# High and low fp32r parts for the product of attention weights with V, query tiles in pairs, masks on GpSimd, and GEMM tiles at low SBUF offsets

## The chip, the cores and the metric

The kernel runs on one core of one Trainium2 chip. The metric is the device time of one execution in microseconds (us); less is better. The core has a matrix engine (TensorE, PE in the profile, with its weight loads as PEld), three elementwise engines (VectorE or DVE, ScalarE or ACT, GpSimd or POOL), a queue engine for transfers (SyncE, SP), an on-chip memory of 128 partitions (SBUF) and the matrix engine's output memory (PSUM, in banks of 128 x 512 float32).

## The reference, cut to what matters

Two layers work on a residual stream x of 512 tokens x 1024 features. Layer 0 mixes tokens with stick-breaking attention, layer 1 with a gated linear recurrence (HGRN2); each is followed by an MLP with squared ReLU. All is float32.

```python
def stick_breaking_attention(q, k, v):
    ...
    for t0 in range(0, seq, Q_BLOCK):                       # query tiles of 128
        t1 = t0 + Q_BLOCK
        z = jnp.einsum('bhqd,bhkd->bhqk', q[:, :, t0:t1], k[:, :, :t1]).astype(jnp.float32) * scale
        causal = jnp.arange(t1)[None, :] < (t0 + jnp.arange(Q_BLOCK))[:, None]
        log_stay = jnp.where(causal, jax.nn.log_sigmoid(-z), 0.0)
        log_between = lax.cumsum(log_stay, axis=3, reverse=True) - log_stay
        weights = jnp.where(causal, jnp.exp(jax.nn.log_sigmoid(z) + log_between), 0.0)
        outs.append(jnp.einsum('bhqk,bhkd->bhqd', weights.astype(v.dtype), v[:, :, :t1]))
...
def squared_relu_mlp(h, w1, w2):
    a = jax.nn.relu(h @ w1)
    return (a * a) @ w2
...
    for layer in range(DEPTH):                              # 2 layers
        h = rmsnorm(x, norm_gains[layer, 0])
        x = x + (stick_breaking_mixer if layer == 0 else hgrn2_mixer)(h, ...)
        h = rmsnorm(x, norm_gains[layer, 1])
        x = x + squared_relu_mlp(h, mlp_w1[layer], mlp_w2[layer])
```

There are 16 attention heads of 64 features; the last line of the loop, attention weights times V, is what the change rewrites.

## The kernel before, in words

**GEMMs on split numbers.** Each large product is made of three fp32r products: an operand is split into a high part (rounded to fp32r) and a low part (the rest), and high x high, high x low and low x high are summed in PSUM. Normed activations are the tiles `xh`, `xl` (tag `P`, 16 buffers of 2 KB a partition), hidden activations `hh`, `hl` and attention outputs `oh`, `ol` (tag `Q`, 16 buffers). Weights come in slabs of 1 MB: two transfers of 512 KB on SP's queue into `wr`, then ACT rounds each half to `wh` (L263) and DVE subtracts to get `wl` (L264), one slab ahead of the matrix engine. Projections with tokens in the output's rows (`gemm_x`) stream 256 weight columns a matmul; those with features in the rows (`gemm_w`) stream 512 tokens.

**Attention.** Four groups g of four heads. In a group the main thread makes q, k (two slabs), norms them, then makes V (a third slab, L533). Two tasks `prepare_pair` transpose q and k and split them (`kst`, `qh`, `ql`); four tasks `head` follow. A head has four query tiles T = 0..3, each of W = 128 (T + 1) keys, and three kinds of step:

- `z_of(T)`: scores `z` by two matmuls, ACT's two sigmoids `sn` and `sg` (L588, L589), a reversed running product over `sn` on DVE (L591), and `sg *= sn` on DVE (L595).
- `turn(T)`: T + 1 transposes of `sg` into PSUM `pa`, and the way back to SBUF `at`: DVE's product with the mask `before` (L610) on the diagonal block, for T > 1 ACT's copy (L609) of the others.
- `apply(T)`: T + 1 float32 matmuls (two passes each in the trace) with 64 columns of V as weights, into the head's half of the partitions of `po`. One PSUM bank `av` holds `po` for the pair; after the second head `split_out` makes `oh`, `ol` (L340, L341).

**What sets the order.** Matmuls are issued in an order fixed by hand: a small planner (`Line`) keeps a clock of nominal matmul times and lets up to three tasks push their steps in between the main thread's GEMM, with the lags in the table `LAG`. DVE, ACT and POOL take the order that the scheduler derives; each engine runs its queue strictly in order. After attention comes `project` (output projection in two parts: part 0 needs heads 0 to 7 and runs beside the last heads, part 1 needs all), then the MLP in four rounds of an up phase (moving tiles `xh`, `xl`) and a down phase (moving tiles `hh`, `hl`), 192 matmuls each.

Of the kernel before, what the change touches and what calls it, by code (L numbers as in the profile page):

```python
# [16 lines left out]
P = 128  # L17
# [13 lines left out]
def level_columns(H, skip):  # L31
# [27 lines left out]
def trunk(  # L59
# [20 lines left out]
    wp = ctx.enter_context(tc.tile_pool(name="wp", bufs=2))  # L80
    ap = ctx.enter_context(tc.tile_pool(name="ap", bufs=2))
# [3 lines left out]
        "P": 16, "Q": 16, "X5": 2, "R4": 4, "B": 2, "qT": 13, "sn": 2, "AT": 3, "sq": 2, "bc": 1,  # L85
# [4 lines left out]
    def sb(tag, shape=(P, S), dt=F32, name=None):  # L90
        return ap.tile(list(shape), dt, tag=tag, bufs=BUFS[tag], name=name or tag)
# [77 lines left out]
    rows = sb("AT", (40, P), name="rows")  # L169
# [6 lines left out]
    def gain(layer, j, kt):  # L176
# [10 lines left out]
    before = cp.tile([P, 2 * P], F32, name="before")  # L187
# [7 lines left out]
    nc.vector.memset(before, 1.0)  # L195
    nc.gpsimd.affine_select(
        out=before[:, P:], in_=before[:, P:], pattern=[[1, P]], compare_op=ALU.is_gt,
        fill=0.0, base=0, channel_multiplier=-1,
    )
    def late_constants():  # L200
        nc.vector.tensor_mul(gqk, gq, gk)
# [45 lines left out]
    def slab_halves(spec):  # L247
# [168 lines left out]
    def attention(norm):  # L416
# [74 lines left out]
        for g in range(4):  # L491
# [27 lines left out]
            vs = []  # L519
            for pair in range(2):  # L520
                shared = {"po": None}
# [4 lines left out]
            V = sb("B", (P, TT, SLAB), name="V")  # L526
            for hf in range(2):
                p = ps("mm")
                for u in range(2):
                    yield from gemm_x(p[:, u * SLAB : (u + 1) * SLAB], wsl, 2 * hf + u, acts)  # L530
                for u in range(2):
                    t = 2 * hf + u
                    nc.scalar.activation(  # L533
                        out=V[:, t, :], in_=p[:, u * SLAB : (u + 1) * SLAB], func=AF.Copy,
                        scale=r[:, t : t + 1],
                    )
            vs.append(V)
        return outs, heads

    live = {"sg": 0}  # L540
# [28 lines left out]
    def head(ready, vs, pair, j, shared, outs, slot):  # L569
# [3 lines left out]
        hc = (2 * pair + j) * SB_DH  # L573
# [6 lines left out]
        def z_of(T):  # L580
# [13 lines left out]
            )  # L594
            nc.vector.tensor_tensor(  # L595
# [3 lines left out]
        at = [None] * TT  # L599

        def turn(T):
            W = (T + 1) * P
# [3 lines left out]
            at[T] = sb("AT", name="at")  # L606
            lead = W - P if T > 1 else 0
            if lead:
                nc.scalar.copy(at[T][:, :lead], p[:, :lead])  # L609
            nc.vector.tensor_mul(at[T][:, lead:W], p[:, lead:W], before[:, 2 * P - (W - lead) :])  # L610

        def apply(T):
            if shared["po"] is None:
                shared["po"] = ps("av", name="po")
            o = blk(shared["po"], T)[j * SB_DH : (j + 1) * SB_DH, :]
            for b in range(T + 1):
                mm(o, vs[0][:, b, hc : hc + SB_DH], blk(at[T], b), b == 0, b == T)

        for step in LAG["head"]:
            if isinstance(step, float):  # L620
                yield step
            else:
                kind, T = step
                while kind == "a" and not vs:
                    yield 0.5
                {"z": z_of, "t": turn, "a": apply}[kind](T)
                if step == ("t", TT - 1):
                    live["sg"] -= 1
        if j == 1:
            outs[slot] = split_out(shared["po"])  # L630
# [304 lines left out]
    def mix(sc, task, V, G, j, outs, slot):  # L935
# [30 lines left out]
        og = sb("AT", name="og")  # L966
# [11 lines left out]
    def store(m, t0, n):  # L978
# [4 lines left out]
        o = sb("AT", name="o")  # L983
# [102 lines left out]
```

## Time and profile before

| | before |
|---|---|
| time, median of 3 runs | 1324.25 us (1322.35 to 1326.43) |
| profiled execution: time / span | 1325.41 us / 1323.7 us |
| PE busy / DVE / ACT / POOL, share of the span | 98% / 60% / 34% / 6% |
| granted matrix clock, mean | 0.996 |
| DMA | 110.64 MB, mean 84 GB/s |

The span is the time from the first to the last instruction of the profiled execution. A busy matrix engine is not one at its peak, since matmuls overlap in the record: what a matmul costs is read from the distance between the starts of successive ones, not from its duration. Rows of a window give, for each engine, its busy time in the window and the number of instructions.

### The profile page before, as it was taken

Reading aid. Unit: us, or ns where it says so; the run is one execution under the profiler, and the core shown is the slowest. Engines: PE = TensorE matmul, PEld = TensorE weight load, DVE = VectorE, ACT = ScalarE, POOL = GpSimd, SP = SyncE. Lnnn points to the kernel's source line nnn. Section 1 sums busy time; section 2 is a strip of 40 time slices with the busy share of each in tenths; the row PEclk is TensorE's granted clock in tenths of the full one; section 3 lists DMA queues with packets and bytes.
Section 4 is the critical chain, followed back from the end, with each engine's and each line's share of the span. In section 5 each row is a group of like instructions: output and inputs, shape, how many; then the busy total and the mean of one; then the engine's idle time right before and its main releaser. Section 6 shows DMA issues by size and latency. Waiting matters only on the chain.

```text
span 1323.7 us, 17619 instructions
## 1 busy us (share of the span) xinstructions
PE 1300.2 (98%) x6993; PEld 1104.2 (83%) x6993; DVE 798.7 (60%) x1534; ACT 446.0 (34%) x756; POOL 80.0 (6%) x139
## 2 busy tenths in 40 slices
PE   7999999999999999999999999999999999999998
PEld 7989898778888888888888888888888888888887
DVE  5787687867535435345578888797764353453441
ACT  5554454544212222123333333342432221221221
POOL 0100000000000000000013222232000000000000
PEclk8999999999999999999999999999999999999999
DMA  5312121113333333333321222221333333333331
GB/s 178 108 33 65 33 68 61 49 48 96 96 96 96 96 96 96 96 96 96 96 89 47 88 64 65 64 65 64 96 96 96 96 96 96 95 96 94 97 96 48
DMA packets 110657, 110.64 MB, mean 84 GB/s; under 512 B 3848, under 2 KB 106416, under 8 KB 110576
## 3 DMA queue, kind: packets, MB, share of 16 engines
q1 hardware_dynamic: 110496, 109.22, 26.7%
q8 instruction: 55, 0.90, 0.3%
q0 software_dynamic: 80, 0.31, 0.1%
q14 instruction: 26, 0.21, 0.0%
HBM read 107.41 MB, written 2.10 MB: 83 GB/s over the span
## 4 chain that ended last, share of the span: by engine, by line
PE 84%; DVE 10%; POOL 2%; issue 2%; ACT 1%; SPq 1%; DMA 1%; DVEq 0%; POOLq 0%; ACTq 0%
PE ps_mm L151 70%; PE po L151 3%; PE ps_z L151 3%; POOL tot L812 2%; DVE sc L845 2%; PE ps_s L151 2%; DVE wl L264 2%; PE pa L155 1%; PE z L151 1%; DVE qr L826 1%; PE po_h L151 1%; PE ps_tr L151 1%; DVE sn L591 1%; DVE X L863 1%; DVE X L867 1%
## 5 line engine op out<-in xcount | busy, mean ns | idle before, releaser
L263 ACT CAST wh<-wr 128x1024 fp32r<-128x1024 f32 x198 | 199.8, 1051 | 399.8 <-PE ps_mm L151 367.8
L264 DVE TENSOR_TENSOR wl<-wr,wh 128x1024 fp32r<-128x1024 f32 x198 | 237.7, 1230 | 17.6 <-ACT wh L263 16.8
L151 PE MATMUL ps_mm<-xh,wh 128*128 128x512 f32 x592 | 232.1, 392 | 0.0
L151 PE MATMUL ps_mm<-xh,wl 128*128 128x512 f32 x592 | 230.5, 389 | 0.0
L151 PE MATMUL ps_mm<-xl,wh 128*128 128x512 f32 x592 | 230.5, 389 | 0.0
L151 PE MATMUL ps_mm<-hh,wh 128*128 128x512 f32 (+1 forms) x520 | 204.1, 393 | 0.0
L151 PE MATMUL ps_mm<-hh,wl 128*128 128x512 f32 (+1 forms) x520 | 203.6, 392 | 0.0
L151 PE MATMUL ps_mm<-hl,wh 128*128 128x512 f32 (+1 forms) x520 | 203.5, 391 | 0.0
L151 PE MATMUL ps_mm<-wh,xh 128*128 128x256 f32 x592 | 173.6, 293 | 0.0
L695 DVE TENSOR_TENSOR xT<-xT,ps_mm 128x512 f32<-128x512 f32 x63 | 43.4, 688 | 213.2 <-PE ps_mm L151 213.2
L151 PE MATMUL ps_mm<-wl,xh 128*128 128x256 f32 x592 | 167.8, 283 | 3.1 <-DVE wl L459 3.1
L151 PE MATMUL ps_mm<-wh,xl 128*128 128x256 f32 x592 | 167.6, 283 | 0.0
L151 PEld LDWEIGHTS ps_mm<-xh,wl 128*128 128x128 f32 x592 | 111.1, 188 | 23.2
L151 PEld LDWEIGHTS ps_mm<-xh,wh 128*128 128x128 f32 x592 | 111.2, 188 | 22.7
L151 PEld LDWEIGHTS ps_mm<-xl,wh 128*128 128x128 f32 x592 | 111.2, 188 | 22.5
L151 PEld LDWEIGHTS ps_mm<-wh,xh 128*128 128x128 f32 x592 | 113.5, 192 | 4.2 <-issue 3.6
L151 PEld LDWEIGHTS ps_mm<-wl,xh 128*128 128x128 f32 x592 | 113.6, 192 | 3.9 <-DVE wl L459 3.3
L151 PEld LDWEIGHTS ps_mm<-hh,wl 128*128 128x128 f32 x520 | 97.6, 188 | 22.9
L151 PEld LDWEIGHTS ps_mm<-hl,wh 128*128 128x128 f32 x520 | 97.7, 188 | 22.7
L151 PEld LDWEIGHTS ps_mm<-hh,wh 128*128 128x128 f32 x520 | 97.7, 188 | 22.6
L672 DVE SCALAR_TENSOR_TENSOR u<-ps_mm,R 128x512 f32<-128x512 f32 x60 | 41.5, 692 | 123.1 <-PE ps_mm L151 123.1
L151 PEld LDWEIGHTS ps_mm<-wh,xl 128*128 128x128 f32 x592 | 113.5, 192 | 0.0
(213 smaller groups left out, 1653.6 us busy)
## 6 DMA issues: line engine op xcount, KB each, us to landing
wr<-in_mlp_w_dram SPq DMA_DIRECT2D x128, 512.0 KB, 3.7
wr<-in_hg_w_in_dram SPq DMA_DIRECT2D x32, 512.0 KB, 3.8
wr<-in_sb_w_qkv_dram SPq DMA_DIRECT2D x22, 512.0 KB, 3.5
wr<-in_sb_w_o_dram SPq DMA_DIRECT2D x8, 512.0 KB, 3.9
wr<-in_hg_w_o_dram SPq DMA_DIRECT2D x8, 512.0 KB, 3.7
xin<-in_x_dram SPq DMA_DIRECT2D x8, 256.0 KB, 5.3
out_dram<-o SPq DMA_DIRECT2D x7, 256.0 KB, 2.3
wr<-in_sb_w_qkv_dram SPq DMA_DIRECT2D x4, 256.0 KB, 5.5
```

The source lines that it names most:

```text
L151: nc.tensor.matmul(o, lhsT=lhsT, rhs=rhs, start=start, stop=stop, **kw)
L155: nc.tensor.transpose(o, in_, ident)
L263: nc.scalar.copy(hi[:, c, :], raw)
L264: nc.vector.tensor_tensor(out=lo[:, c, :], in0=raw, in1=f(hi[:, c, :]), op=ALU.subtract)
L591: nc.vector.tensor_tensor_scan(out=rev, data0=rev, data1=later[:, S - W :][:, ::-1], initial=1.0, op0=ALU.mult, op1=ALU.max,)
L672: nc.vector.scalar_tensor_tensor(out=u, in0=p, scalar=0.0, in1=norm.R, op0=ALU.max, op1=ALU.mult)
L695: nc.vector.tensor_add(xT[m], xT[m], p)
L812: nc.gpsimd.tensor_tensor(out=tots[H][:, :, None], in0=t0, in1=t1, op=ALU.mult)
L826: nc.vector.tensor_tensor(out=q1, in0=q1, in1=t0.to_broadcast([P, S // (2 * H), H]), op=ALU.mult)
L845: nc.vector.copy_predicated(out=o, mask=mask.rearrange("p (g w) -> p g w", g=g)[:, None].to_broadcast([P, 2, g, w]), data=data.rearrange(" ...
L863: nc.vector.tensor_tensor(out=o, in0=qv[:, :, :, part * H : part * H + w], in1=tv[:, :, :, part - 1, None].to_broadcast([P, TT, g, w]), op ...
L867: nc.vector.tensor_tensor(out=C, in0=B[:, :, :, H:], in1=tv[:, :, :, 1, None].to_broadcast([P, TT, g, wc]), op=ALU.mult,)
```

## The change

1. **The product with V.** V is split like the other operands: ACT writes the high part, DVE the low part, side by side, so that one head's 64 high and 64 low columns are 128 columns of weights. `turn` splits the transposed attention weights into `ath` (ACT) and `atl` (DVE), and no longer masks. Query tiles go in pairs: `half` 0 holds T = 0, 1, `half` 1 holds T = 2, 3, their blocks interleaved so that a key block meets both tiles in one matmul of 256 columns; the last key block of a half belongs to the odd tile alone (128 columns). A head has 12 fp32r matmuls in place of 10 float32 ones. The partitions of `po` then hold the sums with V's high and low part, and `gather` adds them (ACT copies one half, DVE adds the other) into a tile `sum`. Each head takes the bank `av` for itself.
2. **Masks.** The diagonal block of `sg` is set to zero above the diagonal by GpSimd's `affine_select`, between the sigmoid and the product on DVE.
3. **Order.** New lags; the main thread waits for the four heads of the group before ahead of its V GEMM (`yield older`), since a group's V now fills both buffers of tag `B`.
4. **SBUF.** Tags `P` and `Q` get a pool of their own (`gp`) that lies below the others. `wr` has two buffers in place of three. Byte offsets in a partition in the two built programs:

| tile | before | after |
|---|---|---|
| `wh`, `wl` | 39296 to 72064 | 38272 to 71040 |
| `P`: `xh`, `xl` | 111232 to 144000 | 79232 to 112000 |
| `Q`: `hh`, `hl`, `oh`, `ol` | 194304 to 227072 | 112000 to 144768 |
| `kst`, `qh`, `ql`, `u` (tag `qT`) | 157440 to 184064 | 182016 to 208640 |
| `sg` (tag `X5`) | 184064 to 194304 | 208640 to 218880 |

```diff
-    "head": [
-        ("z", 0), 0.46, ("z", 1), 2.26, ("z", 2), 1.2, ("t", 0), ("z", 3), 1.5, ("t", 1), ("a", 0),
-        1.54, ("t", 2), ("a", 1), 1.58, ("t", 3), ("a", 2), 1.37, ("a", 3),
-    ],
+    "z": (0.46, 2.26, 1.8),
+    "t": (5.2, 5.0, 4.8, 4.8),
+    "tt": 0.7,
+    "a": (1.6, 2.1),
...
+    gp = ctx.enter_context(tc.tile_pool(name="gp", bufs=16))
...
-            raw = wp.tile([P, h, nc_], F32, tag="wr", bufs=3, name="wr")
+            raw = wp.tile([P, h, nc_], F32, tag="wr", bufs=2, name="wr")
...
+            yield older
+            V = []
             for hf in range(2):
...
+                v = sb("B", (P, 2, 4, 2, SB_DH), dt=F32R, name="V")
...
+                    vh, vl = v[:, u, :, 0, :], v[:, u, :, 1, :]
+                    nc.scalar.activation(out=vh, in_=src, func=AF.Copy, scale=r[:, t : t + 1])
+                    nc.vector.scalar_tensor_tensor(
+                        out=vl, in0=src, scalar=r[:, t : t + 1], in1=f(vh), op0=ALU.mult,
+                        op1=ALU.subtract,
+                    )
...
+            nc.gpsimd.affine_select(
+                out=sg[:, W - P :], in_=sg[:, W - P :], pattern=[[-1, P]], compare_op=ALU.is_gt,
+                fill=0.0, base=0, channel_multiplier=1,
+            )
             nc.vector.tensor_tensor(
                 out=sg[:, : W - 1], in0=sg[:, : W - 1], in1=sn[:, 1:W], op=ALU.mult
             )
...
-            at[T] = sb("AT", name="at")
-            lead = W - P if T > 1 else 0
-            if lead:
-                nc.scalar.copy(at[T][:, :lead], p[:, :lead])
-            nc.vector.tensor_mul(at[T][:, lead:W], p[:, lead:W], before[:, 2 * P - (W - lead) :])
...
+            ah, al = [t[:, 1 - T % 2 :: 2, :] for t in at[half]]
+            src = p[:, :W].rearrange("p (b q) -> p b q", q=P)
+            nc.scalar.copy(ah, src)
+            nc.vector.tensor_tensor(out=al, in0=src, in1=f(ah), op=ALU.subtract)
...
+        def apply(half):
+
+            if not half:
                 shared["po"] = ps("av", name="po")
...
+            n, to = 2 * half + 2, 2 * P * (1 - half)
+            for b in range(n):
+                w = 1 if b == n - 1 else 2
+                for i, t in enumerate(at[half]):
+                    mm(
+                        shared["po"][:, to : to + w * P], vs[0][b // 2][:, b % 2, 2 * pair + j],
+                        t[:, 2 * b : 2 * b + w, :], b + i == 0, b == n - 1 and i == 1,
+                    )
+
+        def gather():
...
+            nc.scalar.copy(to[own], po[other][:, ::-1, :])
+            nc.vector.tensor_tensor(out=to[own], in0=po[own][:, ::-1, :], in1=to[own], op=ALU.add)
...
         if j == 1:
-            outs[slot] = split_out(shared["po"])
+            outs[slot] = split_out(shared["sum"])
```

**How the order moves.** Three places. First the matrix engine's queue in the first group, from the end of one head to the start of the next one's product (`pa` are the transposes of a `turn`, `po` the products with V; "waits" names the engine whose semaphore the instruction waits for). Before, a `turn` and an `apply` of two heads in turn:

```order
L155 MATMUL pa<-ident,sg 128x128 x4
L151 MATMUL po<-at,V 64x128 [waits Activation_49]
L151 MATMUL po<-at,V 64x128
L151 MATMUL po<-at,V 64x128 [waits DVE_49]
L155 MATMUL pa<-ident,sg 128x128 [waits PE_49]
L155 MATMUL pa<-ident,sg 128x128 x2
L151 MATMUL po<-at,V 64x128 x2
```

After, the last matmuls of the first head's `apply(1)`, the second head's `turn(2)`, and its `apply(0)`:

```order
L153 MATMUL po<-ath,V 128x128
L153 MATMUL po<-atl,V 128x128
L157 MATMUL pa<-ident,sg 128x128 [waits PE_49]
L157 MATMUL pa<-ident,sg 128x128
L157 MATMUL pa<-ident,sg 128x128 [waits Pool_49]
L153 MATMUL po<-ath,V 128x256 [waits DVE_49]
L153 MATMUL po<-atl,V 128x256
L153 MATMUL po<-ath,V 128x128
L153 MATMUL po<-atl,V 128x128
```

Both heads now write the one bank `av` in full, so the second one's first product waits for DVE's `sum` of the first, with three transposes in between.

Second, DVE's queue at the same place. Before (`wl` the weight split, `at` the masked copy, `sn` the running product, `sg` the product with it):

```order
L264 TENSOR_TENSOR wl<-wr,wh 128x1024 [waits DMAHW2_49]
L610 TENSOR_TENSOR at<-pa,before 128x128 [waits Activation_49] x2
L591 SCALAR_TENSOR_TENSOR sn<-sn,later 128x128 [waits Activation_49]
L595 TENSOR_TENSOR sg<-sg,sn 128x127 [waits DVE_49,Activation_49]
L610 TENSOR_TENSOR at<-pa,before 128x128 [waits Activation_49]
L591 SCALAR_TENSOR_TENSOR sn<-sn,later 128x256 [waits Activation_49]
```

After:

```order
L620 TENSOR_TENSOR atl<-pa,ath 128x128 [waits Activation_49]
L593 SCALAR_TENSOR_TENSOR sn<-sn,later 128x256 [waits Activation_49]
L601 TENSOR_TENSOR sg<-sg,sn 128x255 [waits DVE_49,Pool_49]
L643 TENSOR_TENSOR sum<-po,sum 64x512 [waits Activation_49]
L620 TENSOR_TENSOR atl<-pa,ath 128x3x128 [waits Activation_49]
L593 SCALAR_TENSOR_TENSOR sn<-sn,later 128x384 [waits Activation_49]
L601 TENSOR_TENSOR sg<-sg,sn 128x383 [waits DVE_49,Pool_49]
```

The `sum` stands behind a running product and an `sg` product, and each `sg` product waits for GpSimd's mask as well.

Third, SP's queue behind the loads of the start (the first rows of `wr` at L256 and L252 are the halves of the second slab). Before:

```order
L1028 DMA gq<-in_sb_q_gain_dram 128x64 [waits DMAHW6_49]
L1029 DMA gk<-in_sb_k_gain_dram 128x64 [waits DMAHW7_49]
L1030 DMA hgain<-in_hg_norm_gain_dram 128x128 [waits DMAHW0_49]
L256 DMA wr<-in_sb_w_qkv_dram 128x4x256 [waits DMAHW1_49]
L256 DMA wr<-in_sb_w_qkv_dram 128x4x256 [waits DMAHW2_49,DVE_49]
```

After:

```order
L1076 DMA gq<-in_sb_q_gain_dram 128x64 [waits DMAHW6_49]
L1077 DMA gq<-in_sb_k_gain_dram 128x64 [waits DMAHW7_49]
L1078 DMA hgain<-in_hg_norm_gain_dram 128x128 [waits DMAHW0_49]
L252 DMA wr<-in_sb_w_qkv_dram 128x4x256 [waits DMAHW1_49,DVE_49]
L252 DMA wr<-in_sb_w_qkv_dram 128x4x256 [waits DMAHW4_49,DMAHW2_49,DVE_49]
```

With two buffers the first half of the second slab waits for a split of the first slab on DVE, and the second half for the split of its last quarter.

More of the change, by code (lines that the diff above doesn't have):

```diff
@@ L619, in head @@
[L619 to L628, printed above, removed]
+            if T % 2 == 0:
+                at[half] = [
+                    sb(f"H{half}", (P, 4 * half + 3, P), dt=F32R, name=n) for n in ("ath", "atl")
+                ]
@@ new lines, in gather, with finish @@
+        def gather():
+            if j == 0:
+                shared["sum"] = sb("qT", name="sum")
+            po, to = [
+                t.rearrange("p (t q) -> p t q", q=P) for t in (shared["po"], shared["sum"])
+            ]
+            nc.scalar.copy(to[own], po[other][:, ::-1, :])
+            nc.vector.tensor_tensor(out=to[own], in0=po[own][:, ::-1, :], in1=to[own], op=ALU.add)
+        def finish(half):
+            while not vs:
+                yield 0.5
+            apply(half)
+            live[half] = 0
```

77 lines of the change are left out of this document (45 added, 32 removed).

## The prediction

> **What bounds the kernel now.** I read the page's busy times first, then the stretches from the first group's query norm to the last head (43.98 to 287.98 us), then the MLP's phases, then the matrix engine's timeline.
>
> ```profile
> PE 1300.2 (98%) x6993; PEld 1104.2 (83%) x6993; DVE 798.7 (60%) x1534; ACT 446.0 (34%) x756; POOL 80.0 (6%) x139
> ...
> core 0: us, PE busy (x) PEld busy (x) DVE busy (x) ACT busy (x) POOL busy (x), PEclk, DMA share, GB/s
> 43.98:97.74 53.76, 52.60 (x406) 47.96 (x404) 45.67 (x90) 29.24 (x64) 2.09 (x4) 1.00 0.23 69
> ...
> 43.98:287.98 244.00, 238.71 (x1710) 208.50 (x1709) 189.22 (x362) 121.05 (x259) 5.74 (x11) 0.99 0.17 55
> ```
>
> The matrix engine is busy 98% of the span: it is the bound, and what leaves it leaves the time, if the others follow. In attention DVE is not far behind: 189.2 of 244 us (78%), in the first group 45.7 of 53.8 (85%). Outside attention it has room.
>
> The MLP's two phases have the same 192 matmuls of 128x512 and differ in the tiles they stream:
>
> ```profile
> 354.34:399.12 44.78, 44.78 (x193) 36.04 (x192) 15.97 (x18) 8.53 (x10) 0.00 (x0) 1.00 0.30 94
> 399.13:442.65 43.52, 43.52 (x193) 36.05 (x192) 22.55 (x30) 12.11 (x16) 0.00 (x0) 1.00 0.32 97
> ...
> 354.34 0.40 PE L151 MATMUL ps_mm<-hh,wh 128*128 128x512 f32 x1
> ...
> 399.13 0.39 PE L151 MATMUL ps_mm<-xh,wh 128*128 128x512 f32 x1
> ...
> 287.47 0.40 PE L151 MATMUL ps_mm<-oh,wl 128*128 128x512 f32 x1
> ...
> 290.27 0.40 PE L151 MATMUL ps_mm<-oh,wl 128*128 128x512 f32 x1
> ```
>
> A down phase (`hh`) takes 44.78 us, an up phase (`xh`) 43.52: 233.2 and 226.7 ns a matmul. The output projection, also on `Q` tiles, has 12 matmuls between its two rows: 2.80/12 = 233 ns. DVE and ACT are busier in the faster phase, so they do not slow the other. What `hh` and `oh` share is their place, offsets from 194304.
>
> **The change part by part.**
>
> *Low GEMM tiles.* `Q` moves into the offsets where `P` lay, all but a shift of 768 bytes. There the rate was 226.7 ns. Eight down phases by 1.26 us are 10.1 us; 288 matmuls of output projections that stand alone (96 of part 1, 192 of the second layer) by 6.6 ns are 1.9. All on the matrix engine, nothing beside it: -12.0 us. If the place is not the cause it is 0; more than 12 no row supports. `P` moves lower, next to the weights. Those are streamed from 39 KB on in `gemm_x`, 256 columns in 0.12 us (rows below), 0.47 ns a column against 0.44 for `xh`: nothing speaks for a cost there, and I take none.
>
> *The product itself.* Before:
>
> ```profile
> 151.89 0.43 PE L151 MATMUL po<-at,V 128*64 128x128 f32 x2
> 152.25 0.39 PE L151 MATMUL ps_mm<-wh,xh 128*128 128x256 f32 x1
> ...
> 154.32 0.87 PE L151 MATMUL po<-at,V 128*64 128x128 f32 x6
> 155.12 0.55 PE L155 MATMUL pa<-ident,sg 128*128 128x128 f32 x3
> 155.59 0.65 PE L151 MATMUL po<-at,V 128*64 128x128 f32 x4
> 156.18 0.39 PE L151 MATMUL ps_mm<-wh,xh 128*128 128x256 f32 x1
> ...
> 157.08 1.09 PE L151 MATMUL po<-at,V 128*64 128x128 f32 x8
> 158.10 0.39 PE L151 MATMUL ps_mm<-wh,xh 128*128 128x256 f32 x1
> 158.32 0.28 PE L151 MATMUL ps_mm<-wl,xh 128*128 128x256 f32 x1
> 158.44 0.28 PE L151 MATMUL ps_mm<-wh,xl 128*128 128x256 f32 x1
> ...
> 315.54 0.95 PE L151 MATMUL ps_st<-ones,acc 128*128 128x1 f32 x8
> ```
>
> From start to next start the four `apply` steps take 0.36, 0.59, 0.80 and 1.02 us, and the first GEMM matmul after one takes 0.22 in place of 0.12, three times a head: 2.77 + 0.30 = 3.07 us. After, eight fp32r matmuls of 256 columns by 0.12 are 0.96; no change of weight width or format is left beside them. Four of 128 columns have no row: at least the 0.11 us that a matmul of one column still takes (`ps_st`: 0.95 for 8, with the last one's tail), at most about the 0.22 of the two float32 passes that they replace. Every fp32r row here has 256 columns or more; I take 0.22, the same width's row. That is 1.84 a head, 16 x 1.23 = -19.7 us; at 0.11 it is -26.7.
>
> *The hand-over of `po`.* Each head now takes the bank that the head before must first leave. A row for that is the last `split_out`:
>
> ```profile
> 286.15 0.82 PE L151 MATMUL po<-at,V 128*64 128x128 f32 x6
> ...
> 287.01 0.59 ACT L340 CAST oh<-po 128x512 fp32r<-128x512 f32 x1 [0.21 <-PE po L151]
> ...
> 286.83 1.22 DVE L264 TENSOR_TENSOR wl<-wr,wh 128x1024 fp32r<-128x1024 f32 x1 [0.15 <-ACT wh L263]
> 287.98 0.68 DVE L341 TENSOR_TENSOR ol<-po,oh 128x512 fp32r<-128x512 f32 x1
> ```
>
> From the last matmul's end (286.97) to DVE's end (288.66) are 1.69 us. In the order eight hand-overs (the second and fourth head of each group) have three transposes ahead, 0.33 us of cover: 1.36 us of waiting each, 2.6 if one more operation like `wl` stands ahead on DVE. I take 1.8, nearer the low end since the queue is not full, and 0.5 for four that have about 2 us of work between: 8 x 1.8 + 4 x 0.5 = +16.4 (10.9 to 27). Behind the waiting product stand GEMM and scores, and so the sigmoids and DVE's next work.
>
> *DVE, ACT, POOL.*
>
> ```profile
> L610 DVE TENSOR_TENSOR at<-pa,before 128x128 f32<-128x128 f32 x48 | 13.5, 285 | 17.9 <-ACT at L609 16.8 <-PE pa L155 0.9
> L610 DVE TENSOR_TENSOR at<-pa,before 128x256 f32<-128x256 f32 x16 | 6.6, 411 | 0.0
> L560 DVE TENSOR_TENSOR kst<-pk,kst 64x512 fp32r<-64x512 f32 x16 | 11.0, 689 | 15.0 <-ACT kst L558 14.6
> L359 DVE SCALAR_TENSOR_TENSOR xl<-ps_x,cols,xh 128x512 fp32r<-128x512 f32 x8 | 5.8, 745 | 3.1 <-ACT xh L358 3.1
> L191 POOL TENSOR_SCALAR_AFFINE_SELECT later<-later 128x128 f32<-128x128 f32 x1 | 0.3, 293 | 0.0
> ...
> L264 DVE TENSOR_TENSOR wl<-wr,wh x198: 1199/1219/1623, 26.7 to 1297.3; 128x1024 fp32r<-128x1024 f32 x198
> ```
>
> A head's `atl` of 128, 256, 384 and 512 columns takes 0.29 + 0.41 + 0.55 + 0.68 = 1.93 us where `at` took 3 x 0.285 + 0.411 = 1.27; `sum` adds 0.69, the low part of V 0.45 (256 columns, between 0.41 and the 0.745 of 512). Together +1.80, by 16 heads 29 us: 218 of DVE's time. The stage becomes 244 - 19.7 + 16.4 + 3, 244 us: 89%, a little above its densest group now. So it is hidden, barely; without the hand-overs it would be 218 of 224 and bound the stage itself. ACT gets five copies a head of at most 0.59: 47 of the 123 us that it has idle. The 64 masks are 18.8 us of POOL, beside a running product in most cases; where the `sg` product follows its own running product directly, DVE waits. DVE's longest `wl`, 1.62 against 1.22, falls where POOL works. Between 0 and 18.8 I take +3, near the low end, because the mask can start when ACT's `sg` is there, usually before the running product ends.
>
> The Trainium skill (SBUF — State Buffer, Who interferes with whom) says that a DVE instruction with two SBUF inputs and a GpSimd instruction that reads SBUF exclude each other for their whole length. By it each mask would hold a DVE operation up or be held up, and the term would go towards 18.8; the row of `wl` agrees in kind (0.4 us).
>
> *Two `wr` buffers.*
>
> ```profile
> 25.47 0.68 DVE L459 TENSOR_TENSOR wl<-wr,wh 128x512 fp32r<-128x512 f32 x1
> ...
> 26.67 2.35 DVE L264 TENSOR_TENSOR wl<-wr,wh 128x1024 fp32r<-128x1024 f32 x2
> ...
> 29.40 0.28 PE L151 MATMUL ps_tr<-wh,xh 128*128 128x256 f32 x1
> ...
> wr<-in_sb_w_qkv_dram SPq DMA_DIRECT2D x22, 512.0 KB, 3.5
> ...
> L263 ACT CAST wh<-wr 128x1024 fp32r<-128x1024 f32 x198 | 199.8, 1051 | 399.8 <-PE ps_mm L151 367.8
> ```
>
> At the start the second slab's second half can be fetched only at 26.15, lands at 29.65, is rounded by 30.70 and split by 31.9. The matrix engine wants it after 12 matmuls, at 30.84: +1.0 us (0 to 2.5, since ACT's queue waits with it). Later ACT's rounding waits for the matrix engine (367.8 us), with the data long there; a load starts one split, about 1.2 us, later in a slab period of 10.9 us (43.52/4): nothing. If DVE fell behind by 3 us, that cover would go.
>
> The sum: -12.0 - 19.7 + 16.4 + 3 + 1.0 = -11.3 us. The profiled run (1325.41, 1.7 us around its span) lies 1.2 above the median, so I put the change on the median: 1324.25 - 11.3 = 1313.
>
> **The rivals.**
>
> *The hand-over is cheap.* At its floor of 10.9 us, with 0.11 for the narrow matmuls and no wait for masks: -26.7 + 10.9 - 12.0 + 1.0, 1297 us. For it: ACT and DVE may find the bank's data first in their queues. Against: DVE would then have to run at 95% (218 of 228 us).
>
> *DVE falls behind and the attention stage grows.* If each of the 12 hand-overs costs 3 us (two operations ahead on DVE, and a mask) in place of 1.4 on average, it is +36, and with 5 us at the masks: -12.0 - 19.7 + 36 + 5 + 1 = +10.3, 1335. Slower begins where hand-overs and masks exceed 35 us together. For it: 89% of DVE, in strict order. Against: in the first group, at 85% of DVE, the matrix engine was busy 52.6 of 53.8 us.
>
> *The low place brings nothing*, and the 6.6 ns belong to something else in the down phase: 1313 + 12, 1325, no change. Against it stands the output projection, another stage with the same tiles and rate. The same section of the skill says that the matrix engine never waits for anyone at SBUF; by it the place would not matter. The 44.78 against 43.52 us speak against that.
>
> **How the numbers follow.** About 0.3%, 4 us, is what this measurement can tell from none: faster is below 1320, slower above 1328. My forecast, 1313 (1305 to 1320 by the bounds of its terms), has 0.50; the cheap hand-over 0.22; DVE behind 0.16, a third of it between 1320 and 1328; the place without effect 0.12, most of it the same. Faster: 0.49 + 0.22 + 0.03 = 0.74; same: 0.01 + 0.05 + 0.08 = 0.14; slower 0.12. The range runs from the cheap hand-over to just below the long stage: 1297 to 1327.
>
> **What would show it.** Down phases of 43.5 us, as long as up phases; if they stay at 44.8 the first term is wrong. `po` matmuls of 256 columns 0.12 us apart, of 128 columns 0.11 to 0.22. Waits of `po` for DVE's `sum` of 1.4 to 2.6 us, eight large ones. DVE at 87 to 92% of a stage of 240 to 246 us; above 95%, or a stage over 255, means the slower rival. `wl` of the second slab holding the matrix engine near 31 us for about 1 us.

## The result and the profile after

The changed kernel takes 1340.2 us (median of 4 runs, 1339.6 to 1341.5) against 1325.3 for the kernel before (4 runs): a ratio of 1.0122, interval 1.0101 to 1.0143. It is slower, by 14.9 us between the medians and 16 us by the ratio, where 11 less were forecast, and outside the range of 1297 to 1327. The profiled run took 1339.64 us, 1337.9 of it span.

The busy times on the page of the changed kernel, then its attention stage and its first down phase in the view by stretches (columns as in the prediction):

```profile
PE 1278.2 (96%) x6865; PEld 1104.8 (83%) x6865; DVE 826.6 (62%) x1565; ACT 466.2 (35%) x804; POOL 116.0 (9%) x202
```

```profile
43.86:313.16 269.30, 226.30 (x1589) 208.70 (x1587) 219.25 (x396) 142.50 (x308) 42.67 (x76) 0.94 0.17 52
...
379.39:422.91 43.52, 43.52 (x193) 36.04 (x192) 15.98 (x18) 8.55 (x10) 0.00 (x0) 1.00 0.31 97
```

The attention stage grew from 244.0 to 269.3 us. Within it the matrix engine was idle 5.3 us before (244.00 - 238.71) and is idle 43.0 now (269.30 - 226.30), and its mean granted clock is 0.94 in place of 0.99. VectorE does the 219 us that were worked out (218), but that is 81% of the longer stage: it is not saturated. The down phase is as long as an up phase, as forecast.

What the matrix engine waited for in that stage (line waited for: total us, times, longest):

```profile
PE po L153 <- DVE sum L643: 15.9, 10, 4.3
PE po L153 <- DVE atl L620: 10.4, 12, 2.2
PE ps_mm L153 <- DVE xT L692: 4.9, 1, 4.9
PE po L153 <- DVE rq_a L224: 4.8, 2, 2.4
PE po L153 <- ACT ath L619: 2.1, 4, 0.7
PE ps_mm L153 <- DVE V L534: 1.7, 1, 1.7
PE ps_mm L153 <- ACT oh L336: 1.7, 1, 1.7
PE z L153 <- ACT sg L591: 1.1, 3, 0.5
```

These are 42.6 us. The bank's hand-over is the first row and also the fourth, though the view names another operation there. `rq_a` is a small step of the next norm, which the product does not read; it ends just behind the addition `sum`, and the view names the one that ended last:

```profile
101.88 0.67 DVE L643 TENSOR_TENSOR sum<-po,sum 64x512 f32<-64x512 f32 x1
102.47 0.16 DVE L224 TENSOR_SCALAR rq_a<-mqk 128x32 int32<-128x32 int32 x1
...
102.69 0.55 PE L153 MATMUL po<-ath,V 128*128 128x256 f32 x1 [2.37 <-DVE rq_a L224]
```

The product starts 0.14 us behind the end of `sum` (102.55), as in the next timeline (156.42 and 156.57), and two_banks and act_release below, where no wait for `sum` is left, have no such row. So the hand-over is 20.7 us in 12 waits. The other six rows, 21.9 us, stood in no term of the sum; `xT` is the addition of the output projection to the residual.

The longest hand-over in the timeline, all engines, in order of start (rows between left out):

```profile
149.98 0.22 PE L153 MATMUL po<-ath,V 128*128 128x128 f32 x1
150.04 0.28 PE L153 MATMUL po<-atl,V 128*128 128x128 f32 x1
150.16 0.41 PE L157 MATMUL pa<-ident,sg 128*128 128x128 f32 x2
...
151.16 0.38 ACT L619 CAST ath<-pa 128x256 fp32r<-128x256 f32 x1
...
151.56 0.58 ACT L642 COPY sum<-po 64x512 f32<-64x512 f32 x1
...
151.69 1.31 DVE L593 TENSOR_TENSOR_SCAN sn<-sn,later 128x512 f32<-128x512 f32 x1
...
154.12 0.66 DVE L601 TENSOR_TENSOR sg<-sg,sn 128x511 f32<-128x511 f32 x1
154.71 0.54 DVE L620 TENSOR_TENSOR atl<-pa,ath 128x384 fp32r<-128x384 f32 x1
155.17 0.54 DVE L601 TENSOR_TENSOR sg<-sg,sn 128x383 f32<-128x383 f32 x1
155.73 0.69 DVE L643 TENSOR_TENSOR sum<-po,sum 64x512 f32<-64x512 f32 x1
...
156.57 0.36 PE L153 MATMUL po<-ath,V 128*128 128x256 f32 x1 [4.26 <-DVE sum L643]
```

The last product starts at 150.04. ScalarE gets to its copy at 151.56, VectorE to its addition at 155.73: it works without a pause from 151.69 on the next scores and `atl`. The bank is free 6.1 us after that product's end near 150.3; the row that the prediction took, `split_out` at the stage's end, gave 1.69: only the end of one `wl` stood ahead in VectorE's queue there, beside ScalarE's copy. The top rows show a good surprise as well: the narrow matmuls are 0.06 and 0.12 us apart, 0.18 for a pair, where 0.22 was taken for one.

### The profile page after: what moved, and what is told of

Read it like the earlier page. It is cut to its first block, busy times and chain, and to the rows that moved or that the text cites. A ratio compares the mean times of both kernels' runs of the same rounds, so it can differ in the third digit from the quotient of the medians.

```text
span 1337.9 us, 17527 instructions
## 1 busy us (share of the span) xinstructions
PE 1278.2 (96%) x6865; PEld 1104.8 (83%) x6865; DVE 826.6 (62%) x1565; ACT 466.2 (35%) x804; POOL 116.0 (9%) x202
## 4 chain that ended last, share of the span: by engine, by line
PE 76%; DVE 14%; issue 3%; ACT 2%; POOL 2%; DMA 1%; SPq 1%; DVEq 0%; ACTq 0%; POOLq 0%
PE ps_mm L153 67%; PE ps_z L153 3%; DVE wl L260 2%; DVE sn L593 2%; POOL tot L861 2%; DVE sc L894 2%; PE ps_s L153 2%; PE po L153 1%; DVE sg L601 1%; DVE qr L875 1%; DVE atl L620 1%; PE po_h L153 1%; DVE X L912 1%; DVE X L916 1%; PE z L153 1%
## 5 line engine op out<-in xcount | busy, mean ns | idle before, releaser
L153 PE MATMUL ps_mm<-xl,wh 128*128 128x512 f32 x592 | 230.4, 389 | 0.0
L153 PE MATMUL ps_mm<-hh,wh 128*128 128x512 f32 (+1 forms) x520 | 201.3, 387 | 0.0
L153 PE MATMUL ps_mm<-hh,wl 128*128 128x512 f32 (+1 forms) x520 | 200.7, 386 | 0.0
L153 PE MATMUL ps_mm<-hl,wh 128*128 128x512 f32 (+1 forms) x520 | 200.6, 386 | 0.0
L153 PEld LDWEIGHTS ps_mm<-hh,wl 128*128 128x128 f32 x520 | 97.6, 188 | 19.7
```

Source lines behind the costliest of these rows:

```text
L153: nc.tensor.matmul(o, lhsT=lhsT, rhs=rhs, start=start, stop=stop, **kw)
```

## The experiments

Each ratio is to the kernel before on the same chip, and a gain in us is the difference of two ratios by 1325 us. These ratios differ by up to 0.13% (1.7 us) from quotients of the medians, so gains of 4 to 6 us are good to about 3 us. The stage, taken from the one profiled run of each kernel, goes from the first group's query norm to the last head's `ol`; "busy" and "idle" are the matrix engine's in it.

| kernel | median us | ratio (95%) | stage | busy | idle |
|---|---|---|---|---|---|
| before | 1325.3 | 1 | 244.0 | 238.7 | 5.3 |
| changed | 1340.2 | 1.0122 (1.0101 to 1.0143) | 269.3 | 226.3 | 43.0 |
| low_only | 1310.6 | 0.9905 (0.989 to 0.992) | 243.4 | 238.1 | 5.3 |
| high_tiles | 1352.2 | 1.0219 (1.0202 to 1.0236) | 269.6 | 227.3 | 42.3 |
| two_banks | 1338.1 | 1.0113 (1.0089 to 1.0137) | 269.5 | 228.9 | 40.6 |
| two_tr | 1353.0 | 1.0221 (1.0202 to 1.024) | 283.5 | 230.4 | 53.1 |
| act_release | 1330.2 | 1.0058 (1.004 to 1.0076) | 259.6 | 220.8 | 38.8 |
| no_atl | 1324.3 | 1.0006 (0.9994 to 1.0018) | 254.3 | 222.1 | 32.2 |
| no_mask | 1341.9 | 1.014 (1.0123 to 1.0157) | 273.2 | 230.9 | 42.3 |
| long_lags | 1335.0 | 1.009 (1.0075 to 1.0105) | 267.7 | 228.4 | 39.3 |
| free_v | 1332.0 | 1.0078 (1.006 to 1.0097) | 263.6 | 226.5 | 37.1 |
| spaced | 1325.8 | 1.0025 (1.0014 to 1.0036) | 256.2 | 221.4 | 34.8 |
| free_long_spaced | 1330.3 | 1.0059 (1.0044 to 1.0074) | 261.6 | 224.0 | 37.6 |
| free_long_spaced_act | 1308.3 | 0.9896 (0.9881 to 0.991) | 239.9 | 215.8 | 24.1 |
| even_no_atl | 1309.1 | 0.989 (0.9875 to 0.9905) | 241.3 | 217.1 | 24.2 |
| even_act_qh | 1302.6 | 0.9845 (0.983 to 0.986) | 233.8 | 214.1 | 19.7 |
| even_act_short | 1316.7 | 0.9947 (0.993 to 0.9964) | 246.2 | 220.0 | 26.2 |
| low_qh | 1306.0 | 0.987 (0.9849 to 0.989) | 239.2 | 237.9 | 1.3 |

**The two halves of the change, apart.** low_only gives the kernel before the low pool; high_tiles takes it from the changed kernel.

```
# low_only, on the kernel before
+    gp = ctx.enter_context(tc.tile_pool(name="gp", bufs=16))
...
-        return ap.tile(list(shape), dt, tag=tag, ...)
+        pool = gp if tag in "PQ" else ap
+        return pool.tile(list(shape), dt, tag=tag, ...)
```

> The kernel before, with only the pool of the GEMM tiles P and Q moved low in SBUF; the attention product is untouched. Theory 1 (the place of the tile that streams sets the matmul's rate, and the loss of the change lies wholly in the attention stage): down phases of 43.5 us, output projection at 227 ns a matmul, 1324.3 - 12 = 1312 to 1314 us. Rival (the low place only pays together with the rest, or costs elsewhere, as in the V and query GEMMs that stream from low weights beside it): 1322 to 1327 us.

> The changed kernel with the P and Q tiles back in the pool where they were; the rest of the change stays. Theory 1 (the two parts of the change add up, and the attention stage lost 25 us): 1340 + 11 = 1350 to 1353 us, attention stage 268 to 272 us. Rival (the tiles' place had a part in the longer attention stage, by way of who shares SBUF with whom): 1340 us or less, stage below 262 us.

The first down phase of low_only, then of high_tiles, in the view by stretches:

```profile
349.66:393.18 43.52, 43.52 (x193) 36.05 (x192) 15.97 (x18) 8.56 (x10) 0.00 (x0) 1.00 0.31 97
```

```profile
381.41:426.19 44.78, 44.78 (x193) 36.04 (x192) 15.96 (x18) 8.53 (x10) 0.00 (x0) 1.00 0.30 94
```

Place alone decides the rate, in either kernel: -12.6 us without the new product (a ratio of 0.9905), and 12.9 lost without the place. The stage stays 269.6 with high tiles, so the halves add, and all of the loss, about 29 us of the whole program (1.0122 against 0.9905), belongs to the rest of the change: product, masks, order and `wr`. Of it 26 us stand in the stage (269.3 against 243.4).

**The bank.** Of eight PSUM banks two_banks gives the product a second one, taken from the transposes; two_tr takes the same bank away and gives nothing.

```
-    PB = {"mm": 2, "z": 2, "tr": 3, "av": 1}
+    PB = {"mm": 2, "z": 2, "tr": 2, "av": 2}    # two_banks
+    PB = {"mm": 2, "z": 2, "tr": 2, "av": 1}    # two_tr
```

> The changed kernel with two PSUM banks for the product and two in place of three for transposes. Theory A (the one bank that a head must get back from the head before costs 16 to 23 us of waits): the waits of the product for `sum` go, stage 246 to 254 us, 1318 to 1326 us, unless the missing transpose bank takes it back (the companion run shows that). Theory B (DVE and ACT are late as such, and the bank is only where it shows): the same time moves to waits for `atl`, `xT` or `sg`, 1335 to 1345 us.

> The changed kernel with one transpose bank fewer and nothing given for it, the control of the run with two product banks. If transposes need their third bank: slower than 1340 us, by 3 to 10 us; if not: 1340 us within 0.2%. The difference between this run and the one with two product banks is the price of the hand-over: theory A 16 to 23 us, theory B under 6 us.

The largest waits of the matrix engine in the stage, of two_tr:

```profile
PE pa L157 <- DVE atl L620: 19.5, 12, 2.6
PE po L153 <- DVE sum L643: 14.8, 10, 4.3
```

Of two_banks:

```profile
PE pa L157 <- DVE atl L620: 21.4, 11, 3.3
PE po L153 <- DVE atl L620: 5.1, 9, 1.0
```

The second bank removes the waits for `sum` (14.8 us, with `rq_a` 21.1) and 14 us of time (1.0221 to 1.0113), a little under theory A; the lost transpose bank costs 13, more than the 3 to 10 expected, since transposes then wait for `atl` to empty theirs. With two_banks alone one would have concluded, wrongly, that the hand-over costs next to nothing (its 1338 us are what theory B forecast). The control gives its price, and the rows show that both kinds of bank are emptied by the same late engine.

**One suspected cost each.** act_release copies both halves out on ScalarE and adds them from SBUF; no_atl and no_mask leave VectorE's and GpSimd's new work out.

```
# act_release
             nc.scalar.copy(to[own], po[other][:, ::-1, :])
-            nc.vector.tensor_tensor(out=to[own], in0=po[own][:, ::-1, :], in1=to[own], op=ALU.add)
+            nc.scalar.copy(mine[own], po[own][:, ::-1, :])
+            nc.vector.tensor_tensor(out=to[own], in0=mine[own], in1=to[own], op=ALU.add)
# no_atl: at[half] holds `ath` alone
-            nc.vector.tensor_tensor(out=al, in0=src, in1=f(ah), op=ALU.subtract)
...
-                for i, t in enumerate(at[half]):
+                for i, t in enumerate(at[half] * 2):
# no_mask
-            nc.gpsimd.affine_select(out=sg[:, W - P :], in_=sg[:, W - P :], ...)
```

> The changed kernel, but both halves of the product's bank are copied out by ScalarE (two copies of 0.58 us), and VectorE adds them from SBUF: the bank comes free without VectorE. Theory A (the price of the hand-over is VectorE's queue: `sum` is late because other work stands ahead of it): waits of the product for the bank fall from 15.9 to 5 to 8 us, 1328 to 1333 us. Theory B (VectorE's lateness reaches the matrix engine anyhow, by `atl` and `xT`): waits for `atl` grow by what `sum` loses, 1337 to 1342 us.

> The changed kernel without the 64 subtractions that make `atl` (31 us of VectorE); the low products read `ath` a second time, so the matrix engine does as much as before and the output loses the low part. Theory B (VectorE, in order and 81% busy, is late with what the matrix engine waits for): all waits shrink, those for `sum` too, stage 236 to 246 us, 1306 to 1317 us. Theory A (the bank's hand-over is what costs): only the 10 us of waits for `atl` go, 1328 to 1332 us.

> The changed kernel without the 64 selections on GpSimd; the diagonal blocks stay unmasked, so the output is another. Theory M (the mask holds the `sg` product up, or VectorE, through the SBUF port; 36 us of GpSimd): 8 to 20 us less, 1320 to 1332 us. Theory A or B (the mask ends beside the running product): 1337 to 1341 us, and the running product 817 ns in place of 838 ns.

The waits of the matrix engine in act_release (two rows) and no_atl (one); then VectorE's scans in the stage, of the changed kernel and of no_mask:

```profile
PE po L153 <- ACT mine L644: 13.2, 11, 2.2
PE po L153 <- DVE atl L620: 12.7, 14, 2.2
```

```profile
PE po L153 <- DVE sum L642: 20.2, 11, 3.2
```

```profile
L593 DVE TENSOR_TENSOR_SCAN sn<-sn,later 128x384 f32<-128x384 f32 (+2 forms) x64 | 53.1, 838 | 14.9 <-ACT sn L590 14.5
```

```profile
L593 DVE TENSOR_TENSOR_SCAN sn<-sn,later 128x384 f32<-128x384 f32 (+2 forms) x64 | 51.9, 818 | 17.5 <-ACT sn L590 16.9
```

act_release gained 8.5 us as theory A has it, but by a smaller step: the bank is waited for 13.2 us in place of 20.7, not 5 to 8. No wait for it is longer than 2.2 us now, in place of 4.3, and busy fell by 5.5 us for the same matmuls (the clock, below). no_atl gained 15 and lies between the theories: without the subtractions VectorE is busy 195.7 us of the stage in place of 219.3, and the waits for `atl` are gone, but those for the bank stay (20.2 in place of 20.7), so the amount of VectorE's work is not the whole cause. The mask costs nothing: 20 ns of each scan, as expected, and no time that shows in the program.

**The order.** long_lags sets larger distances, free_v puts V of every second group on idle `Q` tiles so that its GEMM need not wait for the group before, spaced keeps a head's first product 3.0 us behind the last one of the head before. The fourth, free_long_spaced, does all three.

```
# long_lags
-    "t": (5.2, 5.0, 4.8, 4.8), "tt": 0.7, "a": (1.6, 2.1),
+    "t": (6.2, 6.0, 5.8, 5.8), "tt": 1.0, "a": (3.0, 3.5),
# free_v
-            yield older
...
+                if g % 2:
+                    v = [sb("Q", (P, 4, 2, SB_DH), dt=F32R, name="V") for _ in range(2)]
# spaced, in finish and behind gather
+            while not half and live["free"] > line.at:
+                yield live["free"] - line.at
...
+        live["free"] = line.at + LAG["h"]
```

> The changed kernel with larger distances in its order: a turn 1 us later after its scores, 1.0 in place of 0.7 us between turns, 3.0 and 3.5 in place of 1.6 and 2.1 us from a turn to its product. Theory O (the waits are distances that the order allows too little for, and GEMM could stand in them): PE's waits of 43 us halve, 1318 to 1328 us. Rival (there is no GEMM left to put there, since the heads of a group take as long as its GEMM; later heads only shift the waits to the next group and the end): 1338 to 1350 us.

> The changed kernel with the V tiles of every second group on idle Q tiles, so that the GEMM of V need no longer wait for the last four heads of the group before (that wait came with the change, since the two V tiles of one group now take both `B` buffers). In the order, the fourth head of the first and the third group then has 3.6 us of GEMM around its last turns again, where it stands bare now. Theory O (missing GEMM between the steps of a head is what opens the waits): 4 to 8 us less, 1332 to 1336 us, the 4 us wait for `sum` near 152 us gone. Rival (the waits come from the order inside a group alone): 1338 to 1341 us.

> The changed kernel with one rule more in its order: a head's first product stands at least 3.0 us of the planner's time behind the last product of the head before, so that the bank is free when it comes. Theory A (the price of the hand-over is that it has three transposes ahead): waits for `sum` fall from 15.9 to 2 to 5 us, 1326 to 1331 us. Rival (GEMM is used up earlier in the group and the last head stands barer): the waits move to `atl`, `xT` and the group's end, 1335 to 1342 us.

> Three edits of the order together: V of every second group on Q tiles, the larger distances of turns and products, and 3.0 us between a head's last product and the next head's first. Theory O (the attention stage lost by its order, VectorE has room for 219 us of work): stage 226 to 240 us, waits of the matrix engine under 15 us, 1297 to 1311 us. Theory D (VectorE in strict order cannot be filled above the 85% of the densest stage, whatever the order): stage 252 to 262 us, 1322 to 1333 us.

Waits of the matrix engine in spaced:

```profile
PE po L154 <- DVE atl L621: 15.2, 9, 2.5
PE pk L158 <- DVE qk L511: 8.2, 2, 4.1
...
PE po L154 <- DVE sum L644: 1.5, 2, 0.7
```

Distance does cover the hand-over: in spaced the waits for the bank fall from 20.7 to 1.5 us and the time by 12.9, at the edge of theory A; those for `atl` and `qk` grow, from 10 to 23 us. long_lags gains 4, between its two forecasts, and free_v 6, as theory O had it: its longest wait for `sum` is 3.0 us. All three together gain 8, less than spaced alone, which only theory D allowed, though for another reason than it gave:

```profile
165.93 0.58 ACT L646 COPY sum<-po 64x512 f32<-64x512 f32 x1
...
169.15 0.69 DVE L566 TENSOR_TENSOR kst<-pk,kst 64x512 fp32r<-64x512 f32 x1
169.85 0.69 DVE L569 TENSOR_TENSOR ql<-pq,qh 64x512 fp32r<-64x512 f32 x1
170.56 0.42 DVE L572 CAST qh<-qh 64x512 fp32r<-64x512 f32 x1
171.00 0.68 DVE L647 TENSOR_TENSOR sum<-po,sum 64x512 f32<-64x512 f32 x1
171.82 0.55 PE L154 MATMUL po<-ath,V 128*128 128x256 f32 x1 [4.80 <-DVE sum L647]
...
173.25 0.41 PE L154 MATMUL ps_mm<-wh,xl 128*128 128x256 f32 x1
173.46 0.41 PE L154 MATMUL ps_mm<-wh,xh 128*128 128x256 f32 x1
...
177.03 0.28 PE L154 MATMUL ps_mm<-wh,xl 128*128 128x256 f32 x1
177.09 0.69 DVE L624 TENSOR_TENSOR atl<-pa,ath 128x512 fp32r<-128x512 f32 x1 [5.41 <-ACT ath L623]
177.15 0.29 PE L154 MATMUL ps_mm<-wh,xh 128*128 128x256 f32 x1
```

In this timeline of free_long_spaced `sum` stands in VectorE's queue behind the preparation of the next pair, and the matrix engine waits 4.80 us for it. Then VectorE idles 5.41 us, because its next operation needs ScalarE's copy of transposes that stood in the matrix engine's queue behind that very product, and behind GEMM at the slow rate of the last section. Neither engine is full; they wait for each other in turn.

**Order and release together.** free_long_spaced_act adds act_release to the even order, with 2.2 in place of 3.0 us; even_act_short sets the distances of turns and products back; even_no_atl is the even order, released by VectorE, without `atl`; even_act_qh moves one copy more.

```
# free_long_spaced_act, on free_long_spaced
-    "h": 3.0,
+    "h": 2.2,
...
-            nc.vector.tensor_tensor(out=to[own], in0=po[own][:, ::-1, :], in1=to[own], op=ALU.add)
+            nc.scalar.copy(mine[own], po[own][:, ::-1, :])
+            nc.vector.tensor_tensor(out=to[own], in0=mine[own], in1=to[own], op=ALU.add)
# even_no_atl, on free_long_spaced: as no_atl
-            nc.vector.tensor_tensor(out=al, in0=src, in1=f(ah), op=ALU.subtract)
# even_act_short, on free_long_spaced_act
-    "t": (6.2, 6.0, 5.8, 5.8), "tt": 1.0, "a": (3.0, 3.5),
+    "t": (5.2, 5.0, 4.8, 4.8), "tt": 0.7, "a": (1.6, 2.1),
# even_act_qh, on free_long_spaced_act
-            nc.vector.tensor_copy(qh[i][other, :], f(qh[i][own, :]))
+            nc.scalar.copy(qh[i][other, :], f(qh[i][own, :]))
```

> As the run with three edits, with the bank copied out by ScalarE alone and 2.2 us in place of 3.0 between the products of two heads. If the bank's release by VectorE still costs there: 3 to 8 us less than that run. If the order has covered it: within 2 us of it, or up to 5 us more, since ScalarE has 9 us of copies more.

> The run with three edits of the order, bank released by VectorE, without the 64 subtractions for `atl` (31 us of VectorE); the low products read `ath`, so the output loses the low part. Theory D (the amount of VectorE's work holds the stage): 219 - 31 = 188 us, stage 232 to 242 us, 1300 to 1311 us. Theory Q (`sum` stands in VectorE's queue waiting for ScalarE's copy, with ready work behind it, and this wait does not shrink with the work): `sum` still waits over 10 us, stage 246 to 256 us, 1314 to 1325 us.

> The run with the even order and ScalarE's release (1308 us, VectorE 217 of a 240 us stage), with the 16 copies of `qh` (422 ns each, 6.7 us) moved from VectorE to ScalarE. Theory D (VectorE is now the bound of the stage): 4 to 8 us less, 1300 to 1304 us. Theory Q (waits between the queues, not the amount): 1307 to 1312 us, since ScalarE's 150 us grow to 158 us.

> The run with the even order and ScalarE's release, with the distances of turns and products set back to those of the changed kernel; only the 2.2 us between the products of two heads and the freed V stay of the order's edits. If the larger distances matter: waits for `atl` come back (8 to 12 us), 1314 to 1320 us. If spread and release are what counts: 1305 to 1311 us, the bare end of the last head being shorter.

The stage in free_long_spaced, free_long_spaced_act and even_act_qh, by stretches:

```profile
42.70:304.30 261.60, 224.02 (x1589) 210.53 (x1587) 218.54 (x396) 141.77 (x308) 42.19 (x76) 0.92 0.18 55
```

```profile
42.50:282.40 239.90, 215.81 (x1589) 202.56 (x1588) 217.41 (x396) 149.92 (x324) 43.93 (x76) 0.96 0.19 60
```

```profile
43.40:277.20 233.80, 214.08 (x1588) 201.15 (x1587) 210.33 (x380) 159.69 (x340) 48.10 (x76) 0.97 0.20 62
```

What VectorE waited for at its additions `sum`, in free_long_spaced, free_long_spaced_act and even_no_atl:

```profile
DVE sum L647 <- ACT sum L646: 13.9, 9, 2.7
```

```profile
DVE sum L649 <- ACT mine L648: 3.9, 3, 3.1
```

```profile
DVE sum L646 <- ACT sum L645: 20.7, 9, 5.3
```

The release by ScalarE, with 2.2 in place of 3.0 us, is worth 22 us here, not the 3 to 8 expected: VectorE does nearly the same work, 217 us, in a stage 22 us shorter. No run parts the release from the 0.8 us. Theory D of the even order, that VectorE can't be filled above 85%, falls: it is at 91% here (217.4 of 239.9). In the order the addition also moved behind an `atl` on VectorE, and it waits 3.9 us in place of 13.9. Less work helps too: without `atl` the same order gains as much, 22 us, though VectorE still stands 20.7 us before `sum`, as theory Q said; both theories hold a part. With VectorE at 91%, 6.7 us of copies moved away shortened the stage by 6.1 us, as theory D of that run has it; but the next run gains by the same move with VectorE at 78%, so a bound by the amount is not shown. The distances matter: with the short ones the waits for `atl` are back at 16.0 us and 6.8 us are lost.

**Is it the product?** low_qh makes the same move of `qh` in low_only.

```
# low_qh, on low_only
-            nc.vector.tensor_copy(qh[i][other, :], f(qh[i][own, :]))
+            nc.scalar.copy(qh[i][other, :], f(qh[i][own, :]))
```

> The kernel before with low P and Q tiles (1310.6 us, VectorE 78% of a 243 us stage), with the 16 copies of `qh` on ScalarE. Theory D (VectorE bounds a stage only where it is near 90% of it): no gain, 1309 to 1312 us, so that the 1303 us of the even order are due to the new product. Rival (unloading VectorE helps either kernel alike): 1303 to 1306 us.

Its waits of the matrix engine, and its stage by stretches:

```profile
PE z L153 <- ACT sg L591: 1.3, 4, 0.4
```

```profile
41.80:281.00 239.20, 237.93 (x1716) 208.37 (x1715) 183.14 (x347) 131.58 (x275) 6.21 (x12) 1.00 0.18 56
```

That gained 4.6 us, as the rival has it and against theory D: the waits of 5.2 us that low_only still had are down to the 1.3 of the first row, and the matrix engine is full. So low_qh is at its end, while the new product leaves 214 us of matmuls in place of 238. Of those 24 us even_act_qh has turned 5.4 into a shorter stage (233.8 against 239.2), 1.6 of which its start gives back. It is the fastest kernel run, 0.9845 against 0.987 for low_qh, and the two intervals overlap; that it beats low_only (0.9905) and both kernels of the case is shown.

## Why the prediction was wrong, point by point

*Low GEMM tiles, -12.0.* Right in mechanism and size: 43.52 us a down phase, and 12.6 to 12.9 us by two runs. The rival that the place brings nothing falls. The sentence of the Trainium skill (SBUF — State Buffer, Who interferes with whom) that the matrix engine waits for no one doesn't explain it: the same matmuls on the same tiles took 233 or 227 ns by their place alone.

*The product itself, -19.7.* Right in kind, too small: busy goes from 238.7 to 214.1 in the run with the fewest gaps, -24.6 us. The narrow matmuls were the mis-sized part, 0.18 us a pair where 0.44 was taken, below even the lower end of the range (0.22). By these distances a head takes 0.96 + 0.36 = 1.32 us in place of 3.07, 28.0 us in all (an estimate); the 24.6 still hold some slow matmuls.

*The hand-over, +16.4.* It is 20.7 us in 12 waits, inside the 10.9 to 27. The number of waits was right; that the total came near is partly luck, since the sizes were not: four waits of 2.4 to 4.3 us make 12.8 of it, the other eight are 0.4 to 1.6. I took 1.36 to 2.6 us from a row at the end of the stage, "nearer the low end since the queue is not full"; in the middle of a stage the longest was 4.3. The bank is emptied by two engines in turn, each in strict order, and VectorE had 4 us of other work ahead in the place shown.

*DVE, "hidden, barely".* This is the step that failed. The work was right (219 against 218 us), but a share of 89% was read as room. The waits that I had at nothing are the other 21.9 us of the list, for `atl`, `xT`, `ath`, `V`, `oh` and `sg`; 5.3 us of idle time stood there before. A share says whether an engine's work fits, not whether each piece is ready when an in-order engine comes to it: free_long_spaced and free_long_spaced_act do nearly the same VectorE work, 218 us, and differ by 22 us. The first group before, 85% of VectorE beside a full matrix engine, was taken as proof that such density is harmless; there VectorE freed `po`'s bank once a pair, not once a head.

*The clock.* Not in the sum at all. For the same matmuls busy is 226.3 in the changed kernel and 214.1 in even_act_qh, 12.2 us apart. About half of that is the clock: the trace grants half the clock over 26.1 us of matmuls in the changed kernel's stage, 11.7 in even_act_qh's and 3.4 in the stage before. At 0.21 us in place of 0.12 for 256 columns (last section) three sevenths of such time are lost: 11.2, 5.0 and 1.5 us, an estimate. So the clock cost the change about 10 us. What the other 6 of the 12.2 are is open; the first matmul behind a wait is one candidate (0.19 us to the next start at 156.57, not 0.12), not shown to be all. That 244.0 - 24.6 + 12.2 + 37.7 (idle, 43.0 - 5.3) gives 269.3 is no test, since 24.6 and 12.2 both come from busy.

*Masks, +3.* Nothing: no_mask is not faster. The GpSimd selection did stretch, as the Trainium skill's rule on the shared port (SBUF — State Buffer, Who interferes with whom) says for GpSimd reading SBUF beside VectorE with two inputs there:

```profile
L597 POOL TENSOR_SCALAR_AFFINE_SELECT sg<-sg 128x128 f32<-128x128 f32 x64 | 36.4, 574 | 214.8 <-ACT sg L591 113.2 <-issue 78.8 <-PE z L153 12.2
```

574 ns on average against 293 alone. The trace agrees: a selection that began beside `atl`, with one operand in SBUF, took 0.29 us (at 148.76), one beside `wl`, with two, 1.25 us (at 76.36). GpSimd is the one who waits here, and it has room.

*Two `wr` buffers, +1.0.* Right: a wait of 0.87 us for the second slab's `wl`, and one of 0.48 for a later one at 41.12, where there was none before.

```profile
30.30 0.39 PE L153 MATMUL ps_tr<-wl,xh 128*128 128x256 f32 x1 [0.87 <-DVE wl L260]
```

*Overlooked.* The V tiles of one group now fill both `B` buffers, and `yield older` holds the GEMM of V until the group before is done, so its last head stands bare. free_v puts 6 us on it. It is in the diff, and the order shows it. Nor does any run price the wait for `xT` (4.9 us) alone; in spaced it is 1.1.

*The rivals.* "DVE falls behind and the attention stage grows", 1335 us, is nearest to what happened, by a stage of 269 us (its sign was one over 255). Its other sign, VectorE above 95%, was wrong (81%); its price of hand-overs and masks above 35 us was not reached by those two (20.7 and about 0). It was priced by these alone, not by engines that wait for each other elsewhere, nor by the clock. The cheap hand-over falls with the 20.7 us.

## What to carry to other kernels

Before a PSUM bank is handed through two engines in strict order, price it in the middle of the stage: everything that stands ahead in each of the queues, not the duration of the two copies. A share of busy time below 90% is no proof of cover; look for closed circles (a product waits for a bank, its release for a queue, that queue's head for a transpose behind the product), and break one link: release by the engine with the emptier queue (ScalarE was busy 53% of the stage, VectorE 81%), or place the next use where the release has certainly happened. When a control is cheap, run it: two_banks alone would have shown the wrong thing.

## What the runs showed of the hardware

A gap costs twice. In the timeline of free_long_spaced above, after 4.80 us without work, 256-column matmuls come 0.21 us apart (173.25 to 173.46) in place of 0.12 (177.03 to 177.15), for nearly 5 us. The Trainium skill (TensorE: Matmul & The Clock Gate, HAM oscillation — how this bites in real kernels) says that gaps over about 3.4 us bring this engine back to half its clock; the trace agrees, with 0.21 against 0.12 and a mean granted clock of 0.92 in that stage. The prediction should have drawn on it. But such a gap is not needed: of the six stretches at half clock in the changed kernel's stage, three came behind waits of 4.26, 4.93 and 3.80 us, three behind none longer than 2.4. What the six share is little work just before: in the 3.41 us ahead of each the matrix engine was busy 1.2 us or less (1.20, 1.17, 0.61, 1.03, 1.20 and 0). The stretches last 3.41 us or a multiple. Counted on the grid that they lie on, from 40 us on, all eighteen traces agree: 3.41 us at full clock with under 1.5 us of matmuls were followed by half clock every time, with over 1.9 never. So several waits of 1 to 2 us close together can cost as much as a long one.

The place of the streamed tile in SBUF sets the matmul's rate: 233 ns at the high offsets and 226.7 at the low ones for 128x512, in both kernels, with nothing changed but the pools' place. Why is open; no run here tried other offsets.

Narrow fp32r matmuls are cheap: of a pair of 128 columns the second starts 0.06 us behind the first (149.98 and 150.04) and the next instruction 0.12 behind that, against 0.12 for each of 256 columns.
